# Which pairs take seven products, and where two on-chip columns are copied, in a two-layer encoder trunk

## The chip, the cores and the metric

One Trainium2 chip, one core. TensorE (PE) multiplies, PEld is its weight load, which runs beside it; VectorE (DVE), ScalarE (ACT) and GpSimd (POOL) prepare operands and combine results; SyncE (SP) issues loads. The metric is the device time of one execution, in microseconds, as a median of several runs.

## The reference

x is 256 tokens of 4096 float32 numbers, and there are two layers. A layer normalises x, multiplies it by w_in, runs attention and a retention on the parts, gates both, and multiplies by w_out; a last normalisation follows.

```python
for l in range(DEPTH):                       # DEPTH = 2
    h = rmsnorm(x, norm_w[l])                # (1, 256, 4096)
    proj = h @ w_in[l]                       # 4096 x 11264
    aq, ak, av, ag, rq, rk, rv, rg = jnp.split(proj, SPLIT_POINTS, axis=-1)
    ...                                      # rotary, softmax attention, both retentions, gates
    x = x + jnp.concatenate([a_out, r_out], axis=-1) @ w_out[l]   # 4096 x 4096
return rmsnorm(x, final_norm)
```

## The kernel before

The four large products are four stages: stage 0 is w_in of layer 0, stage 1 its w_out, stages 2 and 3 the same of layer 1. A w_in stage has 11 blocks of 1024 columns (two halves of 512), a w_out stage has four. Rows of a weight matrix come as 16 pairs of 128-row tiles. The work of one pair in one block is a 2 x 2 x 2 problem (two token halves, two k-tiles, two column halves), done in one of two ways:

- with eight products (an "eight"), from two weight pages, A and B;
- with seven (a "seven", from SEVEN_PRODUCTS at lines 160 to 170 of the kernel before), by a scheme like Strassen's, from four pages, A, T, B and U; T and U are sums of weights (`wsum`), which DVE forms in one addition of 128x1024 and two of 128x512.

Each product is one 128x128 by 128x512 product in float32 quality, made of three matmuls: high by high and low of the activations by high of the weights (line 1458), high of the activations by low of the weights (line 1468). So an eight is 24 matmuls and a seven 21. A page becomes a high part, `whi`, by a cast on ACT, and a low part, `wlo`, by a subtraction on DVE (`parts`, line 473). One page in some of the eights is "far": ACT makes `fhi` and its negative `flo`, and an accumulating DMA of POOL's queue adds the weights onto `flo`, so that DVE does nothing for it (`far_parts`). There are one buffer of `fhi` and `flo`, five of the other pages (RING), and five raw loads (RAWS) on SP's queue.

Products add up in seven banks, M1 to M7 (`M` in the rows). `combine` (line 1475) empties them at a block's end into `ca` and `cb`: one copy on ACT and seven additions on DVE. The last of them, ca with M4 or M2, frees the bank that the next block's products need early.

The program is written out by a planner in Python. It keeps clocks of its own (`ve`, `ac`, `now`; costs V_FIXED, S_FIXED, STEP_S, due times LANDING, STORE, FAR_LANDING, margins MARGIN, RUSH, EARLY, ADD_AHEAD, TIGHT_A, TIGHT_B) and between two products (`tick`, line 892) decides with `room` whether one more step of side work may be written at this place. So these constants only set the order of instructions on each engine, and the engines run it in that order.

Between layers, `out_task` (in lines 1518 to 1580) takes each column of 512 of layer 0's result: POOL adds the residual, ACT squares, DVE turns 32x32 blocks into `room`. Columns 0 to 5 go to DRAM and come back as operands. Columns 6 and 7 stay: `move` (line 939) copies `room` back on ACT in 16 copies of 32 partitions, into the tile of the result itself, which the store of x2 must have read by then.

In the profile a helper of line 247 records every instruction of DVE and ACT, so those are told apart by the names of tiles.

Of the kernel before, what the change touches and what calls it, by code (L numbers as in the profile page):

```python
# [12 lines left out]
F32R = mybir.dt.float32r  # L13
# [4 lines left out]
P = 128  # L18
D_MODEL = 4096
SEQ = 256  # L20
# [9 lines left out]
KG = 4  # L30
# [11 lines left out]
STEP_V = 1.6  # L42
STEP_S = 1.3

V_FIXED = 0.15
S_FIXED = 0.12
# [4 lines left out]
LANDING = 11.0  # L51
STORE = 8.0
FETCH = 13.0
FAR_LANDING = 11.0
MARGIN = 0.0

RUSH = 1.5

EARLY = 0.7

ADD_AHEAD = 2.5

# [3 lines left out]

TIGHT_A = 3
TIGHT_B = 5

# [21 lines left out]

FAR_PAIRS = (2, 5, 8, 11, 14)

# [77 lines left out]

SEVENS = (SEVEN, tuple(sorted(SEVEN + MORE)))
EIGHTS = [_p for _p in range(NP) if _p not in SEVENS[1]]

# [3 lines left out]
def pages_of(group, first=False):  # L178

    order, one = [], group[:1]  # L180
    rest = group[1:]
    if first:
        order += [(_p, _k) for _p in NATIVE if _p in group for _k in (PAGE_A, PAGE_B)]
        one = [_p for _p in one if _p not in NATIVE]
        rest = [_p for _p in rest if _p not in NATIVE]
    one = [(_p, _k) for _p in one for _k in (PAGE_A, PAGE_T, PAGE_B, PAGE_U)]
    rest = [(_p, _k) for _p in rest for _k in (PAGE_A, PAGE_B)]
    for _i, _v in enumerate(one):
        order += [_v] + rest[_i : _i + 1]
    return order + rest[len(one) :]  # L190


def is_far(group, p, k):

    return k == PAGE_B and p in FAR_PAIRS


def slots_of(group, second, first=False, plain=False):

    for _p, _k in pages_of(group, first):  # L200
        if _p in SEVENS[second] and not (first and _p in NATIVE):
            yield [(_b, _p, (ALL, _a), _k, _h) for _b, _a, _pg, _h in SEVEN_PRODUCTS if _pg == _k]
# [10 lines left out]
EASY = ("M7",)  # L213

TOGETHER = 4
BANKS = ("M1", "M2", "M3", "M4", "M5", "M6", "M7", "M8")

# [44 lines left out]
def hybrid_encoder(  # L262
# [136 lines left out]
    class Weights:  # L399


        def __init__(self):
            self.pages = []
            for l in range(DEPTH):
                for w, n in ((w_in, N_IN), (w_out, N_OUT2)):
                    for b in range(n):
                        second = w is w_out
                        for g in GROUPS[second]:
                            start = (l, b) == (0, 0) and w is w_in
                            for slot in slots_of(g, second, start):  # L410
# [3 lines left out]
                                one.seven = one.pair in SEVENS[second] and not one.whole  # L414
                                one.far = is_far(g, one.pair, one.kind) and not (
                                    start and (g in GROUPS[0][:2] or one.whole)
# [164 lines left out]
    def dead_room():  # L581

        if not rooms:
            e, o = len(EIGHTS), len(SEVENS[1])
            kinds = {
# [5 lines left out]
            }  # L591
            order = "x7h x7l x3 x3 x7h x7l x7h x7l x3 x8h x8l x7h x7l x3 x8h x8l x7h x7l x3 x7h" if MORE else "x3 x3 x8h x8l x3 x3 x8h x8l x7l x7h x3 x3 x8h x8l x3 x3 x8h x8l x7l x7h"
            rooms.extend(kinds[v] for v in order.split())
        tag, bufs, shape, flat = rooms.pop(0)
# [19 lines left out]
    def split_pair(p, v, whole, stage):  # L614
# [14 lines left out]
        x0, x1 = v[:, 0], v[:, 1]  # L629
        if p in SEVENS[stage % 2]:  # L630
            while sums_of or held[0] + pledged() >= PAGES:
# [3 lines left out]
            sums_of.append(p)  # L635
            hi = t(ap, [P, 7, P], "x7h", len(SEVENS[1]), F32R)
            lo = t(ap, [P, 7, P], "x7l", len(SEVENS[1]), F32R)
            f = page([P, 5, P], "xf")
# [15 lines left out]
        else:  # L654
# [5 lines left out]
            else:  # L660
                both = [t(ap, [P, 7, P], v, len(SEVENS[1]), F32R) for v in ("x7h", "x7l")]
                hi, lo = (v[:, 0:4, :].rearrange("p (i m) t -> p i (m t)", m=MT) for v in both)
# [24 lines left out]
        version[p] += 1  # L687
        operand[p] = (hi, lo) if p in SEVENS[stage % 2] else (hi, lo, g)
        operand_at[p] = max(ve.until, ac.until) + PASS
# [657 lines left out]
    def block(after_pair, phase, then, first_order=False, order=LAST_ORDER, last=None, plain=False, hurried=False):  # L1347
# [6 lines left out]
        flat = []  # L1354
        second = phase % 2 == 0
        rush[0] = RUSH if hurried else 0.0
        for g in GROUPS[second]:
            for slot in slots_of(g, second, first_order, plain):
                flat += slot
# [24 lines left out]
        def begin_product(n, name, p, index, k, h):  # L1384
# [18 lines left out]
            if first_order and p in NATIVE:  # L1403
                a = as_it_comes[p][0][:, index[0], index[1] * P : (index[1] + 1) * P]
            elif p in SEVENS[second]:
                a = at(operand[p], *index, ALL)
# [114 lines left out]
    def out_task(l, n, res):  # L1521
# [29 lines left out]
        else:  # L1551
            yield LANDING - 2.0
            to = res.rearrange("p m n -> p (m n)")
            yield from move(turn, to)
            drop()
            put(n, to, 2 * l + 2)

    def out_tasks(l, n, c):
        for i in range(2):
            nc.gpsimd.dma_start(c[i], residual(l, 2 * n + i), accum_op=ALU.add)  # L1560
        yield LANDING
        for i in range(2):
            yield from out_task(l, 2 * n + i, c[i])

# [242 lines left out]
```

## Time and profile before

| what | us |
|---|---|
| median of 3 runs | 2627.58 (2625.68 to 2627.82) |
| the profiled execution, its own time | 2625.96 |
| its span in the trace | 2623.8 |
| PE busy | 2601.0 (99%) |
| DVE busy | 2166.6 (83%) |
| ACT busy | 1804.2 (69%) |
| POOL busy | 372.9 (14%) |

The difference between the profiled execution's time and its span, 2.16 us, lies around the span. In the trace stage 0 ends near 985 us, stage 1 near 1317, stage 2 near 2280, and the last matmul of stage 3 starts at 2611.99. PE is nearly always busy, so its time is to be read by where its matmuls start later than one after another; the busy shares of the other engines tell how near they are to being late for it.

### The profile page before, as it was taken

How to read it: one execution, taken by the hardware profiler on the slowest of the kernel's cores; microseconds unless marked ns; L12 is line 12 of the kernel's file. 1: busy time of each engine (PE TensorE's matmuls, PEld its weight loads, DVE VectorE, ACT ScalarE, POOL GpSimd, SP SyncE). 2: the span in 40 equal slices, each digit the busy share in tenths (PEclk: the TensorE clock that was granted, in tenths of full speed). 3: DMA queues.
4: the chain of work that ended last, by engine and by line, in shares of the span. 5: the costliest groups of instructions: out<-in, count | busy, mean ns of one | idle time of the engine just before them, and what ended most of it. 6: DMA issues, size and time to landing. Idle time of an engine off the chain costs nothing.

```text
span 2623.8 us, 34532 instructions
## 1 busy us (share of the span) xinstructions
PE 2601.0 (99%) x11725; PEld 2154.2 (82%) x11725; DVE 2166.6 (83%) x2684; ACT 1804.2 (69%) x2576; POOL 372.9 (14%) x510
## 2 busy tenths in 40 slices
PE   9999999999999999999999999999999999999998
PEld 7788888888888888888878888888888888888886
DVE  7898887798778898877978878888887688987876
ACT  8676676667565788655877666776576557876655
POOL 0012211221111101111111111211210111010000
PEclk9999999999999999999999999999999999999999
DMA  9988888887778777889988888888877787788887
GB/s 305 285 262 285 272 271 284 270 269 243 235 238 249 239 249 237 274 262 281 311 246 259 271 274 283 266 273 288 280 231 217 245 258 239 221 259 264 254 249 228
DMA packets 201121, 683.94 MB, mean 261 GB/s; under 512 B 24176, under 2 KB 30832, under 8 KB 200944
## 3 DMA queue, kind: packets, MB, share of 16 engines
q1 hardware_dynamic: 147760, 521.27, 56.3%
q0 software_dynamic: 53184, 160.46, 26.5%
q8 instruction: 92, 1.51, 0.2%
q14 instruction: 85, 0.70, 0.1%
HBM read 637.60 MB, written 44.04 MB: 260 GB/s over the span
## 4 chain that ended last, share of the span: by engine, by line
PE 92%; issue 1%; DMA 1%; ACT 1%; DVE 1%; POOL 0%; POOLq 0%; DVEq 0%; ACTq 0%
PE M L1458 59%; PE M L1468 30%; PE ps L973 1%; PE ps L974 1%; PE ps L975 1%; DMA q<-q_dram 1%; PE ps L1458 0%; DMA wraw<-in_w_in 0%; DVE wlo L247 0%; ACT ca L247 0%; DVE ca L247 0%; PE ps L1468 0%; DVE cb L247 0%; ACT pr L247 0%; ACT whi L247 0%
## 5 line engine op out<-in xcount | busy, mean ns | idle before, releaser
L247 ACT CAST whi<-wraw 128x1024 fp32r<-128x1024 f32 (+1 forms) x808 | 768.7, 962 | 463.0 <-PE M L1458 310.3
L247 DVE TENSOR_TENSOR wlo<-wraw,whi 128x1024 fp32r<-128x1024 f32 (+1 forms) x808 | 886.9, 1110 | 236.6 <-ACT whi L247 230.9
L1458 PE MATMUL M<-whi,x8h 128*128 128x512 f32 x1340 | 521.9, 389 | 0.0
L1458 PE MATMUL M<-whi,x8l 128*128 128x512 f32 x1340 | 521.5, 389 | 0.0
L1458 PE MATMUL M<-whi,x7h 128*128 128x512 f32 x1265 | 493.9, 390 | 3.7 <-DVE ca L247 2.5
L1458 PE MATMUL M<-whi,x7l 128*128 128x512 f32 x1265 | 492.9, 390 | 0.0
L247 ACT CAST whi<-wsum 128x1024 fp32r<-128x1024 f32 x314 | 329.6, 1050 | 137.1 <-PE M L1458 93.8
L1468 PE MATMUL M<-wlo,x8h 128*128 128x512 f32 x1340 | 420.2, 389 | 0.0
L247 DVE TENSOR_TENSOR wlo<-wsum,whi 128x1024 fp32r<-128x1024 f32 x314 | 382.5, 1218 | 38.7 <-ACT whi L247 36.8
L1468 PE MATMUL M<-wlo,x7h 128*128 128x512 f32 x1265 | 407.8, 389 | 1.1 <-DVE wlo L247 1.1
L1458 PEld LDWEIGHTS M<-whi,x8h 128*128 128x128 f32 x1340 | 251.6, 188 | 51.7 <-issue 0.2
L1458 PEld LDWEIGHTS M<-whi,x8l 128*128 128x128 f32 x1340 | 251.6, 188 | 51.7 <-issue 0.2
L1468 PEld LDWEIGHTS M<-wlo,x8h 128*128 128x128 f32 x1340 | 251.2, 188 | 51.7
L1458 PEld LDWEIGHTS M<-whi,x7h 128*128 128x128 f32 x1265 | 237.8, 188 | 55.7 <-DVE ca L247 2.9
L1468 PEld LDWEIGHTS M<-wlo,x7h 128*128 128x128 f32 x1265 | 237.5, 188 | 50.5 <-DVE wlo L247 1.5
L1458 PEld LDWEIGHTS M<-whi,x7l 128*128 128x128 f32 x1265 | 238.0, 188 | 48.9
L1458 PE MATMUL M<-whi,x 128*128 128x512 f32 x840 | 258.9, 389 | 0.7 <-ACT whi L247 0.7
L505 POOL DMA_DIRECT2D flo<-in_w_in x108 | 97.3, 901 | 1044.4 <-ACT flo L247 1001.4
L247 ACT CAST fhi<-wraw 128x1024 fp32r<-128x1024 f32 (+1 forms) x148 | 154.7, 1045 | 99.8 <-PE M L1458 93.9
L247 DVE TENSOR_TENSOR wsum<-wraw 128x1024 f32<-128x1024 f32 x157 | 191.2, 1218 | 18.7 <-DMA wraw<-in_w_out 11.3
L1458 PEld LDWEIGHTS M<-whi,x 128*128 128x128 f32 x840 | 157.1, 188 | 32.9 <-ACT whi L247 1.1
L1458 PE MATMUL M<-fhi,x8h 128*128 128x512 f32 x440 | 171.3, 389 | 0.0
(301 smaller groups left out, 3282.9 us busy)
## 6 DMA issues: line engine op xcount, KB each, us to landing
wraw<-in_w_in SPq DMA_DIRECT2D x700, 512.0 KB, 5.0
wraw<-in_w_out SPq DMA_DIRECT2D x256, 512.0 KB, 5.2
flo<-in_w_in POOLq DMA_DIRECT2D x108, 512.0 KB, 7.9
flo<-in_w_out POOLq DMA_DIRECT2D x38, 512.0 KB, 8.8
full<-next_dram POOLq DMA_DIRECT2D x18, 512.0 KB, 7.7
p_dram<-room POOLq DMA_DIRECT2D x64, 128.0 KB, 4.6
pT<-p_dram POOLq DMA_DIRECT2D x16, 512.0 KB, 8.1
next_dram<-room POOLq DMA_DIRECT2D x40, 128.0 KB, 5.9
```

Of the source, the lines that this page charges most:

```text
L247: return call(out, *args, **kwargs)
L505: nc.gpsimd.dma_start(g.lo[h], g.src[0][:, h, :], accum_op=ALU.add)
L973: nc.tensor.matmul(out, a[0], b[0], start=start, stop=False)
L974: nc.tensor.matmul(out, a[0], b[1], start=False, stop=False)
L975: nc.tensor.matmul(out, a[1], b[0], start=False, stop=stop)
L1458: nc.tensor.matmul(acc[name], a[i], g.hi[h], start=m == first[name] and not i, stop=False)
L1468: nc.tensor.matmul(acc[name], a, g.lo[h], start=False, stop=m == final[name])
```

## The change

Before, the pairs 0, 3, 6, 9, 12 are sevens in the w_in stages, and 0, 1, 3, 6, 9, 12 in the w_out stages. After it each stage has a list of its own: 0, 3, 6, 9, 11 in stage 0, and 0, 3, 6, 9, 11, 13 in the others. The far pages are those of pairs 2, 5, 8, 12 and 14 in stage 0 and 2, 5, 8, 12 and 15 in the others (before: 2, 5, 8, 11, 14 in all). The on-chip columns 6 and 7 are copied from `room` to a page of their own, `to`, as soon as the turn is written, and column 7 is timed by its own residual. Constants of the planner change. The operands' tiles for retention rooms (`dead_room`) are listed pair by pair. The names TURNS, APART and ABREAST have values under which they change nothing.

```diff
-STEP_S = 1.3
-V_FIXED = 0.15
+STEP_S = 1.0
+V_FIXED = 0.08
...
-SEVEN = (0, 3, 6, 9, 12)
-MORE = (1,)
-DELAYED = tuple([_p for _p in range(NP) if _p not in SEVEN + MORE][-5:])
+SEVEN0 = (0, 3, 6, 9, 11)
+SEVEN1 = (0, 3, 6, 9, 11, 13)
+SEVEN2 = (0, 3, 6, 9, 11, 13)
+SEVEN3 = (0, 3, 6, 9, 11, 13)
+SEVENS = (SEVEN0, SEVEN1, SEVEN2, SEVEN3)
+MIXED = tuple(sorted(set(SEVEN0 + SEVEN1 + SEVEN2 + SEVEN3)))
+DELAYED = tuple([_p for _p in range(NP) if _p not in MIXED][-5:])
...
-FAR_PAIRS = (2, 5, 8, 11, 14)
+FAR0 = (2, 5, 8, 12, 14)
+FAR1 = (2, 5, 8, 12, 15)
...
+FARS = (FAR0, FAR1, FAR2, FAR3)
...
-def is_far(group, p, k):
-    return k == PAGE_B and p in FAR_PAIRS
+def is_far(stage, p, k):
+    return k == PAGE_B and p in FARS[stage] and p not in SEVENS[stage]
...
+OTHER = True
...
         else:
-            yield LANDING - 2.0
-            to = res.rearrange("p m n -> p (m n)")
-            yield from move(turn, to)
-            drop()
+            if OTHER:
+                yield 0.0
+                to = page([P, KG * SEQ], "to")
+                yield from move(turn, to)
+                drop(2)
+            else:
...
             put(n, to, 2 * l + 2)
 
     def out_tasks(l, n, c):
         for i in range(2):
             nc.gpsimd.dma_start(c[i], residual(l, 2 * n + i), accum_op=ALU.add)
-        yield LANDING
-        for i in range(2):
-            yield from out_task(l, 2 * n + i, c[i])
+            if i < 1:
+                yield APART
+        second = now.t + LANDING
+        yield max(0.0, LANDING - APART)
+        one = out_task(l, 2 * n, c[0])
+        if n < N_OUT2 - 1 or not ABREAST:
+            yield from one
+            yield max(0.0, second - now.t)
+            yield from out_task(l, 2 * n + 1, c[1])
+            return
```

How the order on the engines moves is shown at three places, each in the order of one engine's instructions. `x4` stands for four such instructions in a row.

First, ACT where stage 1 has passed into stage 2: `room` to `ca` are the copies of an on-chip column, `room,sums<-cb` the squares of the other column (cb is the second column of the last block). Before:

```order
L247 CAST whi<-wraw 128x1024 x2
L247 CAST whi<-wsum 128x1024
L247 COPY ca<-room 32x256 x8
L247 CAST whi<-wraw 128x1024
L247 COPY ca<-room 32x256 x4
L247 CAST whi<-wraw 128x512
L247 COPY ca<-room 32x256 x4
L247 CAST fhi<-wraw 128x1024
L247 ACTIVATE flo<-fhi 128x1024
L247 ACTIVATE room,sums<-cb 128x512 x2
L247 CAST whi<-wraw 128x1024
L247 CAST whi<-wsum 128x1024
```
After:

```order
L263 COPY to<-room 32x256 x4
L263 CAST whi<-wsum 128x1024
L263 COPY to<-room 32x256 x4
L263 CAST whi<-wraw 128x1024
L263 COPY to<-room 32x256 x4
L263 CAST whi<-wraw 128x1024
L263 CAST whi<-wsum 128x1024
L263 COPY to<-room 32x256 x4
L263 CAST whi<-wraw 128x1024
L263 CAST whi<-wraw 128x512
L263 ACTIVATE room,sums<-cb 128x512 x2
L263 ACTIVATE to<-to,nw 128x8x32 x4
```
Before, the 16 copies stand in runs of eight, four and four, and the squares of cb come behind them and behind a far page's `fhi` and `flo`. After, the copies (into `to`) stand in fours between casts, and the squares of cb come two casts behind the last of them, with no far page ahead.

Second, DVE at the end of the seventh block of stage 2 (columns of rg and rv; `D` and `wTl` belong to a retention, M_16482 is the bank that frees last). Before:

```order
L247 TENSOR_TENSOR cb<-ca,M_16566 128x512
L247 TENSOR_TENSOR ca<-cb,M_16450 128x512
L247 TENSOR_TENSOR wsum<-wraw,wsum 128x512
L247 TENSOR_TENSOR wsum<-wsum,wraw 128x512
L247 TENSOR_TENSOR wlo<-wsum,whi 128x1024
L247 TENSOR_TENSOR wTl<-D,wTh 128x1024
L247 TENSOR_TENSOR cb<-cb,M_16454 128x512
L247 TENSOR_TENSOR cb<-ca,M_16472 128x512
L247 TENSOR_TENSOR cb<-cb,M_16472 128x512
L247 TENSOR_TENSOR ca<-ca,M_16478 128x512
L247 TENSOR_TENSOR wlo<-wraw,whi 128x1024
L247 TENSOR_TENSOR ca<-ca,M_16482 128x512
```
After (that bank is M_16537 here):

```order
L263 TENSOR_TENSOR wlo<-wraw,whi 128x1024
L263 TENSOR_TENSOR wlo<-wsum,whi 128x1024
L263 TENSOR_TENSOR cb<-ca,M_16615 128x512
L263 TENSOR_TENSOR ca<-cb,M_16508 128x512
L263 TENSOR_TENSOR wlo<-wraw,whi 128x512
L263 TENSOR_TENSOR wTl<-D,wTh 128x1024
L263 TENSOR_TENSOR cb<-cb,M_16512 128x512
L263 TENSOR_TENSOR cb<-ca,M_16522 128x512
L263 TENSOR_TENSOR cb<-cb,M_16522 128x512
L263 TENSOR_TENSOR ca<-ca,M_16531 128x512
L263 TENSOR_TENSOR wlo<-wraw,whi 128x1024
L263 TENSOR_TENSOR ca<-ca,M_16537 128x512
```
The same combining additions stand there. After the change four `wlo` stand in the stretch where two stood, one of them the half page of a seven's page B, and the two `wsum` halves come before it.

Third, DVE at the end of the first block of stage 0. Before:

```order
L247 TENSOR_TENSOR wsum<-wraw 128x1024
L247 TENSOR_TENSOR wlo<-wraw,whi 128x1024
L247 TENSOR_TENSOR x_264<-x3f,x_264 128x256
L247 TENSOR_TENSOR wlo<-wraw,whi 128x1024
L247 TENSOR_TENSOR cb<-ca,M_457 128x512
L247 TENSOR_TENSOR ca<-cb,M_380 128x512
L247 TENSOR_TENSOR cb<-ca,M_372 128x512
L247 TENSOR_TENSOR cb<-cb,M_372 128x512
L247 TENSOR_TENSOR wsum<-wraw,wsum 128x512
L247 TENSOR_TENSOR wsum<-wsum,wraw 128x512
L247 TENSOR_TENSOR wlo<-wsum,whi 128x1024
L247 TENSOR_TENSOR x3f<-x8h 128x256
```
After:

```order
L263 TENSOR_TENSOR cb<-ca,M_454 128x512
L263 TENSOR_TENSOR ca<-cb,M_376 128x512
L263 TENSOR_TENSOR cb<-ca,M_368 128x512
L263 TENSOR_TENSOR cb<-cb,M_368 128x512
L263 TENSOR_TENSOR wsum<-wraw 128x1024
L263 TENSOR_TENSOR wlo<-wraw,whi 128x1024 x2
L263 TENSOR_TENSOR x3f<-x8h 128x256
L263 TENSOR_TENSOR x3f<-x8l 128x256
L263 TENSOR_TENSOR x3f<-x3f 128x256
L263 TENSOR_TENSOR wlo<-wraw,whi 128x1024
L263 TENSOR_TENSOR wsum<-wraw,wsum 128x512
L263 TENSOR_TENSOR wsum<-wsum,wraw 128x512
```
Before, the `wsum<-wraw` of the next block's first seven and the two `wlo` behind it stand ahead of the combining additions; after, the four additions of M6, M7 and M5 stand ahead of them. The last additions of M3 into cb come behind the rows shown in both, before with one x3f group between, after with two.

Counted over the program, 33 of the matmuls of 128x512 go (one product in each of 11 blocks). DVE gets 22 more `wlo<-wsum` of 128x1024, 11 more `wsum<-wraw` of 128x1024 and 22 more `wsum` of 128x512; ten `wlo` of 128x1024 become ten of 128x512. ACT gets 22 more `whi<-wsum` of 128x1024, and ten `whi` of 128x1024 become ten of 128x512. SP's loads stay as many, and POOL issues one more transfer.

## Rows read from the trace of the kernel before

**Rows 1.** Page, busy time and 40 slices of granted clock

```profile
PE 2601.0 (99%) x11725; PEld 2154.2 (82%) x11725; DVE 2166.6 (83%) x2684; ACT 1804.2 (69%) x2576; POOL 372.9 (14%) x510
...
PEclk9999999999999999999999999999999999999999
```
**Rows 2.** Chain that ended last: start us, us, what, xcount

```profile
188.41 1.81 PE M L1458 x8
```
**Rows 3.** Waits of PE: line, releaser: us in total, times, longest

```profile
PE M L1468 <- DVE wlo L247: 2.8, 2, 1.7
PE M L1458 <- DVE ca L247: 2.5, 3, 1.0
PE ps L973 <- ACT pr L247: 2.0, 2, 1.0
```
**Rows 4.** Timeline 84 to 103: start, duration, engine, operation, [wait, releaser]

```profile
88.39 1.05 ACT L247 CAST whi<-wraw 128x1024 fp32r<-128x1024 f32 x1 [4.52 <-DMA wraw<-in_w_in]
...
95.85 0.50 PE L1468 MATMUL M<-wlo,x7h 128*128 128x512 f32 x1 [1.06 <-DVE wlo L247]
...
97.58 0.50 PE L1458 MATMUL M<-whi,x7h 128*128 128x512 f32 x1 [1.23 <-DVE cb L247]
...
98.46 0.63 PE L1458 MATMUL M<-whi,x7h 128*128 128x512 f32 x1
...
101.45 0.52 PE L1458 MATMUL M<-whi,x7l 128*128 128x512 f32 x1
```
**Rows 5.** Timeline 1340 to 1362, ACT, DVE and PE

```profile
1343.20 3.32 ACT L247 COPY ca<-room 32x256 f32<-32x256 f32 x8
1353.66 0.61 ACT L247 ACTIVATE room<-cb 128x512 f32<-128x512 f32 x1
1355.01 0.17 DVE L247 TENSOR_REDUCE rstd<-sums 128x2 f32<-128x16 f32 x1 [4.37 <-ACT room L247]
1355.97 0.73 PE L1458 MATMUL M<-whi,x 128*128 128x512 f32 x2 [0.71 <-ACT whi L247]
1359.83 0.50 PE L1468 MATMUL M<-wlo,x 128*128 128x512 f32 x1 [1.75 <-DVE wlo L247]
```
**Rows 6.** Timeline 1314 to 1325, DVE: starts of instructions in a row

```profile
1315.18 0.68 DVE L247 TENSOR_TENSOR cb<-cb,M 128x512 f32<-128x512 f32 x1
1315.78 0.68 DVE L247 TENSOR_TENSOR ca<-ca,M 128x512 f32<-128x512 f32 x1
...
1322.79 1.22 DVE L247 TENSOR_TENSOR wsum<-wraw 128x1024 f32<-128x1024 f32 x1
1323.92 1.22 DVE L247 TENSOR_TENSOR wlo<-wraw,whi 128x1024 fp32r<-128x1024 f32 x1
```
**Rows 7.** Timeline 1927 to 1932: end of the seventh block of stage 2

```profile
1930.05 0.68 DVE L247 TENSOR_TENSOR ca<-ca,M 128x512 f32<-128x512 f32 x1
...
1931.92 0.39 PE L1458 MATMUL M<-whi,x7h 128*128 128x512 f32 x1
```
**Rows 8.** Windows: PE, PEld, DVE, ACT, POOL busy (x), clock, DMA share, GB/s

```profile
900.00:1000.00 100.00, 100.00 (x458) 83.24 (x457) 94.80 (x145) 83.20 (x137) 13.81 (x14) 1.00 0.72 227
...
2000.00:2100.00 100.00, 100.00 (x454) 83.27 (x453) 74.67 (x81) 60.05 (x69) 8.72 (x12) 1.00 0.74 230
```
**Rows 9.** Timeline 1329 to 1333: a far page is cast and sent, ACT and POOL

```profile
1329.91 1.05 ACT L247 CAST fhi<-wraw 128x1024 fp32r<-128x1024 f32 x1 [0.36 <-PE M L1458]
1331.00 1.06 ACT L247 ACTIVATE flo<-fhi 128x1024 fp32r<-128x1024 f32 x1
1332.35 0.86 POOL L505 DMA_DIRECT2D flo<-in_w_in  x1 [4.08 <-ACT flo L247]
```
**Rows 10.** Tile flo, 900 to 1000: its transfers

```profile
DMA to landing us min/median/max: 6.2/9.3/9.9
```
**Rows 11.** Tile flo, 2000 to 2100: its transfers

```profile
DMA to landing us min/median/max: 5.4/7.0/8.3
```
**Rows 12.** Timeline of PE at the end

```profile
2611.99 0.39 PE L1468 MATMUL M<-x7h,x8h 128*128 128x512 f32 x1
```

More of the change, by code (lines that the diff above doesn't have):

```diff
@@ L170 @@
 ]
-SEVENS = (SEVEN, tuple(sorted(SEVEN + MORE)))
-EIGHTS = [_p for _p in range(NP) if _p not in SEVENS[1]]
+EIGHTS = [_p for _p in range(NP) if _p not in MIXED]
 GROUPS = [[tuple(range(_a, _b)) for _a, _b in zip(_s, _s[1:] + (NP,))] for _s in SEVENS]
@@ L187, in pages_of, with slots_of @@
     rest = [(_p, _k) for _p in rest for _k in (PAGE_A, PAGE_B)]
+    turns = TURNS if group[-1] == NP - 1 else "0123"
     for _i, _v in enumerate(one):
-        order += [_v] + rest[_i : _i + 1]
-    return order + rest[len(one) :]
-def is_far(group, p, k):
-    return k == PAGE_B and p in FAR_PAIRS
-def slots_of(group, second, first=False, plain=False):
+        order += [_v] + [rest.pop(0) for _j in turns if _j == str(_i) and rest]
+    return order + rest
+def is_far(stage, p, k):
+    return k == PAGE_B and p in FARS[stage] and p not in SEVENS[stage]
+def slots_of(group, stage, first=False, plain=False):
     for _p, _k in pages_of(group, first):
-        if _p in SEVENS[second] and not (first and _p in NATIVE):
+        if _p in SEVENS[stage] and not (first and _p in NATIVE):
             yield [(_b, _p, (ALL, _a), _k, _h) for _b, _a, _pg, _h in SEVEN_PRODUCTS if _pg == _k]
@@ L213 @@
 EASY = ("M7",)
+APART = 0.0
 TOGETHER = 4
+OTHER = True
+TURNS = "0123"
+ABREAST = False
 BANKS = ("M1", "M2", "M3", "M4", "M5", "M6", "M7", "M8")
@@ L413, in __init__ @@
                                 one.whole = start and one.pair in NATIVE
-                                one.seven = one.pair in SEVENS[second] and not one.whole
-                                one.far = is_far(g, one.pair, one.kind) and not (
+                                one.seven = one.pair in SEVENS[stage] and not one.whole
+                                one.far = is_far(stage, one.pair, one.kind) and not (
                                     start and (g in GROUPS[0][:2] or one.whole)
@@ L591, in dead_room @@
             }
-            order = "x7h x7l x3 x3 x7h x7l x7h x7l x3 x8h x8l x7h x7l x3 x8h x8l x7h x7l x3 x7h" if MORE else "x3 x3 x8h x8l x3 x3 x8h x8l x7l x7h x3 x3 x8h x8l x3 x3 x8h x8l x7l x7h"
-            rooms.extend(kinds[v] for v in order.split())
+            for p in range(NP):
+                if p not in EIGHTS:
+                    rooms.extend(kinds[v] for v in ("x7h", "x7l"))
+                else:
+                    rooms.extend(kinds[v] for v in ("x3", "x8h", "x8l")[: 3 if p in EIGHTS[2:] and p not in DELAYED else 1])
         tag, bufs, shape, flat = rooms.pop(0)
@@ L1354, in block @@
         flat = []
-        second = phase % 2 == 0
+        stage = phase - 1
         rush[0] = RUSH if hurried else 0.0
-        for g in GROUPS[second]:
-            for slot in slots_of(g, second, first_order, plain):
+        for g in GROUPS[stage]:
+            for slot in slots_of(g, stage, first_order, plain):
                 flat += slot
@@ L1560, in out_tasks @@
             nc.gpsimd.dma_start(c[i], residual(l, 2 * n + i), accum_op=ALU.add)
-        yield LANDING
-        for i in range(2):
-            yield from out_task(l, 2 * n + i, c[i])
+            if i < 1:
[8 more added lines that the diff above has]
+            return
+        yield next(one)
+        yield max(0.0, second - now.t)
+        two = spawn(out_task(l, 2 * n + 1, c[1]))
+        yield from one
+        while not two.done:
+            yield 0.5
     def last_combine(res):
```

43 lines of the change are left out of this document (25 added, 18 removed).

## The prediction, made before the changed kernel ran

> **What bounds the kernel now.** I read the page first. PE is busy for 99% of the span and its clock stands at full in all 40 slices, while DVE has 83% and ACT 69% [rows 1]. The chain of waits agrees: its longest pieces are eight matmuls each, 1.81 us, so 0.226 us from one start to the next [rows 2]. A matmul that goes is therefore worth 0.226 us, as long as DVE and ACT still bring each page and free each bank in time. What PE loses now is in the waits of PE [rows 3] and, around them, in starts that lie further apart than 0.226 us. Start by start, less 0.226 us each, these places lose: about 4.7 us at the end of the first block, near 97; 1.0 at the end of the second, near 185; 4.6 in the attention of layer 0; 1.6 where stage 1 passes into stage 2, near 1317; 3.1 at 1356 to 1360; 1.1 where stage 2 passes into stage 3, near 2280; 1.4 at the start. That is 17.5 us of 2612, the whole that better order could give back. Then the timelines of the two largest places [rows 4, 5], DVE's spacing [rows 6], an end of a block in stage 2, where DVE gets the new work [rows 7], and the windows with the far pages' landings [rows 8, 10, 11].
>
> **What goes from PE.** 11 blocks of stage 2 lose one product of three matmuls: 33 x 0.226 = 7.5 us. All stand in PE's row of work, so they count in full where nothing else comes late. After the last matmul's start at 2611.99 [rows 12] 11.8 us of the span are left, and that end is written as before: 0.
>
> **What DVE and ACT get.** Starts in a row are 0.60 us apart for 128x512 and 1.13 for 128x1024 [rows 6]. DVE: 22 x 1.13 + 11 x 1.13 + 22 x 0.60, and 10 x (0.60 - 1.13), is 45.2 us, all in stage 2: 4.1 us for each of its blocks of some 87 us (stage 2 is 963 us). ACT gets 22 casts, at about 1.09 from one start to the next [rows 9] 24 us, less five for the halved ones: 1.7 us a block. DVE's share in stage 2 goes from about 83% to 88%. A stretch of 100 us near the start of stage 1 already has DVE at 94.8% with PE full throughout [rows 8], so as a share this fits. What hides it is DVE's idle time between pages; where that is gone is at the ends of blocks, below.
>
> **The copies of the on-chip columns.** Before, ACT runs eight copies from 1343.20 on, then four and four, then a far page, and starts the squares of cb only at 1353.66. DVE's first reduction behind them waits 4.37 us, to 1355.01, and the `wlo` in its queue behind that wait with it. PE then waits 0.71 us for a `whi` and 1.75 for a `wlo` [rows 5], and with the matmuls around them loses 3.1 us. After, no run of copies is longer than four, and the far page no longer stands ahead of the squares. DVE's wait goes, and of those behind it the `wlo` come in their turn. I take 3.1 off. Bounds: 0, if the squares are late by something else (column 7 now goes by its own residual), and 3.2, all that is lost there. The two orders differ at just the instructions that waited, so I take the end that these rows are near to.
>
> **The end of the first block.** A cast waits 4.52 us for a load at 88.39, DVE's subtraction waits for the cast, and all combining additions stand behind it; so PE waits 1.06 us for a `wlo` and 1.23 for a cb. From 98.46 to 101.45 its seven next starts are 0.43 apart, near the 0.427 of the clock's lower level, 1.2 GHz [rows 4]. After, four of the additions stand ahead of those weights. But the last two cb have one x3f group more between them. I expect about half, 2.5 us; bounds 0 and 4.8. The end of the second block follows with 0.5 of its 1.0 (0 to 1.0). Attention's waits (ACT `pr`, [rows 3], and others) are for its own chain, which is the same after: 0, bounds 2 more and 4.6 less, since side work around it is placed anew.
>
> **Ends of blocks in stage 2.** The bank freed last is needed by the next block's page B. In before, at the seventh block, ca with the last bank starts at 1930.05 and takes 0.68, and the product that needs it starts at 1931.92 [rows 7]: 1.2 us to spare. DVE's queue there, from the retention's last `D`, is 4 x 1.13 + 10 x 0.60 = 10.5 us, against 60 matmuls by 0.226 = 13.6 us on PE; after, 4 x 1.13 + 11 x 0.60 = 11.1 against 49 matmuls, 11.1: late by the time of handing over. Counted so, four further ends keep 1.1 us where they had 2.0 to 2.4, and six stay near 1.8 to 2.0. I add 1.5 us in stage 2: one end late by 0.5 to 1, and one or two of those with 1.1 late by a little. Bounds: 0, and the rival below. Where stage 1 passes into 2 and 2 into 3, the same count goes from 1.9 and 1.3 to 0.3; both places already wait on DVE's ca (2.5 us in three waits [rows 3]). I add 0.3 each, 0.6 together (0 to 3).
>
> **Far pages.** There is one buffer, so the next far page is cast only when PE has left the last. From there to its need stand mostly 65 matmuls, 14.7 us, before; after, 53 (12.0 us) in five blocks of stage 0, and 59 or 60 (13.5) in some sixteen others. The cast starts at 1329.91 and POOL issues at 1332.35 [rows 9]: 2.4 us. The median landing is 9.3 us with DVE at 94.8% [rows 8, 10] and 7.0 with DVE at 74.7% at nearly the same DMA share [rows 8, 11]. So 11.7 us against 12.0 at the median, and the longest, 9.9, is 0.3 late. I add 1.0: about three of the five late by 0.3. Bounds: 0, and 5 x 0.3 with 1.4 for the lower clock behind two of them, as in [rows 4], 4.3. By those rows 20 points of DVE's share go with 2.3 us of landing, so the 5 points in stage 2 give 0.6 us, which the 13.5 there hold.
>
> The Trainium skill, SBUF — State Buffer, section Who interferes with whom, says that the only contention is between VectorE and GpSimd over a shared port pair, and that DMA has ports apart from all engines. By that rule a busier DVE delays no landing, and the term for far pages in stage 2 is nothing; by the rows it is 0.6 us a page, inside the margin. The sum is the same by both, except in the slower rival, which it would make a little less likely. The trace agrees with neither firmly, since the two stretches also differ in what else they load.
>
> **Sum.** -7.5 - 3.1 - 2.5 - 0.5 + 1.5 + 0.6 + 1.0 = -10.5 us on the profiled execution's 2625.96: 2615.5. The median of the runs, 2627.58, lies 1.6 above that execution; on it, 2617.1. I say 2617.
>
> **Rivals.** A measurement of this kernel can tell 0.2%, 5.3 us: faster is under 2622.3, slower above 2632.8.
>
> *The saving is eaten by new waits.* All of the 7.5 us stands, the copies give their 3.1, but the first block gives nothing, and late banks and far pages cost 7 in all. For it: in stage 2 the end that I could follow has no spare time left, and five blocks of stage 0 have far pages within 0.3 us. Against it: the margins that the rows show were each above 1 us. Sum -7.5 - 3.1 + 7 = -3.6: 2624.
>
> *Nearly all waits go.* The planner's order holds everywhere: -7.5 - 3.1 - 4.8 - 1.0 and 1.3 to 2 of the other losses, with nothing added: -18, 2609.5. For it: block ends stay above 1 us at ten of eleven. Against it: three different places would have to come out at their best.
>
> *DVE becomes the bound at the ends of stage 2's blocks (slower).* The mechanism is the bank: DVE comes to ca with the last bank behind one `wlo` more, at each of the 11 ends. It decides as soon as DVE's queue at an end is longer by one 1.13 us subtraction than my count, for the 1.1 us that four ends have and the 1.2 that [rows 7] show are then gone. A wait like those of [rows 4], 1.2 us, and the matmuls at half clock behind it, 7 x 0.2 = 1.4, make 2.6 us an end; at the ends that have least (five) 13 us, at all eleven 29. With -7.5 - 3.1 that is 2630 to 2646; I say 2636. For it: the new work stands in DVE's queue just there, with DVE at 88%. Against it: [rows 8], 94.8% without a wait of PE, and the place near 1360, which lost only 0.6 us more than its two waits, so 2.6 is the dear end.
>
> The Trainium skill, TensorE: Matmul & The Clock Gate, Part 1, has the clock fall to half once PE has idled and come back when it is busy. The spacing of 0.43 at 98.46 agrees; near 1360 [rows 5] waits of 0.71 and 1.75 us cost little beside themselves, so a wait of that size need not bring it.
>
> That the change doesn't do what it says can be left out: the 33 matmuls are gone from the order of PE.
>
> **Chances.** My forecast 0.62, nearly all waits go 0.12, eaten 0.18, slower 0.08. Of my forecast's 0.62 some 0.04 reaches above 2622.3. The eaten case is within 0.2%, and a quarter of the slower case, whose cheap end is 2630, stays there too. So faster 0.62 - 0.04 + 0.12 = 0.70; same 0.04 + 0.18 + 0.02 = 0.24; slower 0.06. The range leaves out half of the best case and the dear half of the slower one: 2609 to 2630. My forecast's own range is 2611 to 2622.
>
> **What would show it.** PE's matmul count falls by 33, and stage 2 is about 6 us shorter. Near 1356 the waits for `whi` and `wlo` are gone, and DVE's reduction of rstd waits under 1 us. Near 97 one of the two waits is left, and the starts of 0.43 are fewer. In stage 2 the waits of PE show one to three on DVE's ca, under 1 us each, and in stage 0 perhaps three on flo. I am wrong if waits on ca or `wlo` come at most ends of stage 2, or if a new one of over 2 us shows in attention, or if the copies leave the squares as late as they were.

## The result, and the profile after

The changed kernel takes 2631.59 us (median of 14 runs, 2627.81 to 2635.59), the kernel before 2625.68 on the same chips (14 runs, 2621.0 to 2629.26): a ratio of 1.0024, 95% interval 1.0017 to 1.0031. The forecast was 2617, 0.4% faster. The profiled execution has a span of 2629.6 us against 2623.8.

The page and the chain of what ended last, by engine. PE is still busy for 99%, but DVE and DMA now hold 5% of the chain, where they held 2% before. The first two of these rows answer to [rows 1].

```profile
PE 2598.5 (99%) x11692; PEld 2149.6 (82%) x11692; DVE 2210.1 (84%) x2740; ACT 1829.4 (70%) x2599; POOL 367.1 (14%) x511
...
PEclk9999999999999999999999999999999999999999
...
PE 92%; DVE 3%; DMA 2%; ACT 1%; issue 1%; POOL 0%; DVEq 0%; SPq 0%; POOLq 0%; ACTq 0%
```
The waits of PE in the changed kernel: line, releaser: us in total, times, longest. They answer to [rows 3]. The waits on ACT's `pr` in attention are gone; waits on `flo`, on operands `x` and on DVE's ca are new or longer.

```profile
PE M L1477 <- DVE ca L263: 6.4, 5, 2.6
PE M L1487 <- DMA flo<-in_w_in: 4.2, 2, 3.3
PE M L1477 <- DVE x L263: 2.9, 2, 1.7
PE M L1487 <- DVE wlo L263: 1.8, 4, 0.9
PE M L1487 <- DMA flo<-in_w_out: 1.1, 1, 1.1
```
Worked out over all matmuls (start less the start before, less 0.2267 us, the usual distance of two starts), what PE loses at each place, in us:

| place (us in the span of before) | before | after | the forecast's term |
|---|---|---|---|
| end of the first block (60 to 115) | 4.5 | 1.2 | -2.5 |
| far page in the second block (115 to 150) | 0 | 5.2 | far pages +1.0 in all |
| end of the second block (150 to 320) | 1.3 | 0.1 | -0.5 |
| attention of layer 0 (320 to 560) | 4.9 | 0.6 | 0 |
| end of stage 0, blocks of stage 1 (960 to 1245) | 0.4 | 2.2 | none |
| last 70 us of stage 1 (1245 to 1316) | 0.1 | 5.0 | none |
| stage 1 into 2 (1316 to 1336) | 1.5 | 4.5 | +0.3 |
| on-chip columns (1336 to 1365) | 3.0 | 0 | -3.1 |
| operands x of stage 2 (1365 to 1420) | 0 | 1.9 | none |
| ends of blocks in stage 2 (1420 to 2240) | 0.7 | 1.9 | +1.5 |
| stage 2 into 3 (2240 to 2310) | 1.2 | 4.9 | +0.3 |
| operands x of stage 3 (2310 to 2390) | 0 | 2.3 | none |
| everywhere, the first 60 us too | 18.9 | 31.2 | |

So PE loses 12.3 us more, has 7.5 us of matmuls less, and the stretch behind its last matmul's start, 12.8 us, is 1.0 longer: +5.8, as the spans differ. The last matmul now starts at 2616.80, where [rows 12] had 2611.99.

A place in a single trace can differ from the next execution's by some 2.5 us. The trace of the kernel with one transfer moved (below), whose orders on PE, ACT, DVE and SP are the same as here, loses 2.7 us in attention where this one loses 0.6, and 2.5 in the last 70 us of stage 1 where this one loses 5.0. The passages between stages (4.8 and 4.8) and the operands x (2.3 and 2.0) agree in both.

**Where the on-chip columns are copied.** ACT and DVE: the last four copies, into `to`, come at 1348.78, the squares of cb at 1351.93, and DVE's reduction at 1353.29 shows no wait where [rows 5] had 4.37 us. PE waits for nothing between 1340 and 1362.

```profile
1348.78 1.65 ACT L263 COPY to<-room 32x256 f32<-32x256 f32 x4
...
1351.93 0.63 ACT L263 ACTIVATE room<-cb 128x512 f32<-128x512 f32 x1
...
1353.29 0.17 DVE L263 TENSOR_REDUCE rstd<-sums 128x2 f32<-128x16 f32 x1
```
**The far page in the second block.** POOL's queue, then PE: the transfer of `flo` is issued behind the four stores of vh and vl; PE waits 3.29 us for it, and behind it the starts from 129.51 to 132.92 lie 0.43 apart (3.41 us in eight steps); the granted clock there is 0.50, the lower of the two levels, as in [rows 4]. The row of the tile gives its landing, the longest of two, 12.1 us. The kernel before issues it ahead of the stores, which the first two rows show.

```profile
118.17 0.91 POOL L505 DMA_DIRECT2D flo<-in_w_in  x1 [3.70 <-ACT flo L247]
118.76 1.91 POOL L1281 DMA_DIRECT2D kv_dram<-vh  x2
```
The changed kernel:

```profile
113.27 1.59 POOL L1300 DMA_DIRECT2D kv_dram<-vh  x2 [1.06 <-ACT vh L263]
114.83 1.50 POOL L1300 DMA_DIRECT2D kv_dram<-vl  x2
116.30 0.97 POOL L521 DMA_DIRECT2D flo<-in_w_in  x1
...
128.48 0.50 PE L1487 MATMUL M<-flo,x8h 128*128 128x512 f32 x1 [3.29 <-DMA flo<-in_w_in]
...
129.51 0.62 PE L1477 MATMUL M<-whi,x7h 128*128 128x512 f32 x1
...
132.92 0.40 PE L1477 MATMUL ps<-whi,x8h 128*128 128x512 f32 x1
...
DMA to landing us min/median/max: 8.5/10.3/12.1
```
**The end of stage 2.** DVE, then PE. PE waits 2.57 us, for `ca<-cb,M`, which empties bank M7: the next block's second product is on M7. DVE runs from 2263.95 to 2284 without a gap, so that addition comes when its queue comes to it. Behind the wait the starts from 2279.99 to 2282.98 are 0.43 apart, at a granted clock of 0.50. In the kernel before M7 is emptied in time, and PE waits 0.86 us, for the last bank:

```profile
2274.50 0.69 DVE L247 TENSOR_TENSOR ca<-cb,M 128x512 f32<-128x512 f32 x1
...
2280.06 0.47 PE L1458 MATMUL M<-whi,x7h 128*128 128x512 f32 x1 [0.86 <-DVE ca L247]
```
The changed kernel:

```profile
2263.95 0.43 DVE L263 TENSOR_TENSOR full<-full 128x256 f32<-128x256 f32 x1
...
2276.97 0.68 DVE L263 TENSOR_TENSOR cb<-ca,M 128x512 f32<-128x512 f32 x1
2277.68 0.69 DVE L263 TENSOR_TENSOR ca<-cb,M 128x512 f32<-128x512 f32 x1
...
2278.51 0.47 PE L1477 MATMUL M<-whi,x7h 128*128 128x512 f32 x1 [2.57 <-DVE ca L263]
...
2279.99 0.63 PE L1477 MATMUL M<-whi,x7l 128*128 128x512 f32 x1
...
2282.98 0.55 PE L1477 MATMUL M<-whi,x8l 128*128 128x512 f32 x1
```
**Stage 1 into 2.** Here too PE waits for M7, 1.96 us. In the kernel before (first row) DVE empties it ahead of the sums of a seven's page U; in the changed kernel it does so behind them and their `wlo`.

```profile
1310.92 0.69 DVE L247 TENSOR_TENSOR ca<-cb,M 128x512 f32<-128x512 f32 x1
...
1318.60 0.69 DVE L263 TENSOR_TENSOR ca<-cb,M 128x512 f32<-128x512 f32 x1
...
1319.44 0.47 PE L1477 MATMUL M<-whi,x7h 128*128 128x512 f32 x1 [1.96 <-DVE ca L263]
```
**The seventh block of stage 2.** [rows 7] had 1.2 us to spare here. Now ca with the last bank is added at 1932.54, and PE waits 0.43 us for it: this term came as forecast.

```profile
1932.54 0.68 DVE L263 TENSOR_TENSOR ca<-ca,M 128x512 f32<-128x512 f32 x1
...
1933.28 0.50 PE L1477 MATMUL M<-whi,x8h 128*128 128x512 f32 x1 [0.43 <-DVE ca L263]
```
**The operands x.** DVE at the start of stage 3: the sums of a seven's page U (the second of the two is shown) and its `wlo` stand ahead of the split of the operand x that PE has been waiting for; the wait is 1.69 us.

```profile
2350.33 0.69 DVE L263 TENSOR_TENSOR wsum<-wsum,wraw 128x512 f32<-128x512 f32 x1
2350.93 1.22 DVE L263 TENSOR_TENSOR wlo<-wsum,whi 128x1024 fp32r<-128x1024 f32 x1
2352.07 0.75 DVE L263 TENSOR_TENSOR x8l<-ca,x8h 128x256 fp32r<-128x256 f32 x2
2352.86 0.42 DVE L263 TENSOR_TENSOR ca<-ca 128x256 f32<-128x256 f32 x1
2353.20 0.42 DVE L263 TENSOR_TENSOR x<-ca,x 128x256 fp32r<-128x256 f32 x1
...
2353.67 0.50 PE L1477 MATMUL M<-whi,x 128*128 128x512 f32 x1 [1.69 <-DVE x L263]
```

### The profile page after: what moved, and what is told of

Read it like the earlier page. It is cut to its first block, busy times and chain, and to the rows that moved or that the text cites. A ratio compares the mean times of both kernels' runs of the same rounds, so it can differ in the third digit from the quotient of the medians.

```text
span 2629.6 us, 34599 instructions
## 1 busy us (share of the span) xinstructions
PE 2598.5 (99%) x11692; PEld 2149.6 (82%) x11692; DVE 2210.1 (84%) x2740; ACT 1829.4 (70%) x2599; POOL 367.1 (14%) x511
## 4 chain that ended last, share of the span: by engine, by line
PE 92%; DVE 3%; DMA 2%; ACT 1%; issue 1%; POOL 0%; DVEq 0%; SPq 0%; POOLq 0%; ACTq 0%
PE M L1477 59%; PE M L1487 29%; DVE wlo L263 2%; PE ps L993 1%; PE ps L992 1%; PE ps L994 1%; DMA flo<-in_w_in 1%; DMA wraw<-in_w_in 1%; DVE wsum L263 1%; PE ps L1477 0%; PE M L1471 0%; DMA flo<-in_w_out 0%; ACT whi L263 0%; DVE cb L263 0%; PE ps L1487 0%
## 5 line engine op out<-in xcount | busy, mean ns | idle before, releaser
L263 DVE TENSOR_TENSOR wlo<-wsum,whi 128x1024 fp32r<-128x1024 f32 x336 | 409.5, 1219 | 119.3 <-ACT whi L263 118.7
L263 ACT CAST whi<-wsum 128x1024 fp32r<-128x1024 f32 x336 | 352.5, 1049 | 125.2 <-PE M L1477 93.5
L263 DVE TENSOR_TENSOR wsum<-wraw 128x1024 f32<-128x1024 f32 x168 | 204.5, 1217 | 15.3 <-DMA wraw<-in_w_out 10.8
L1477 PE MATMUL M<-fhi,x8l 128*128 128x512 f32 x438 | 170.5, 389 | 0.0
```

The lines of the kernel that those rows point to most:

```text
L263: return call(out, *args, **kwargs)
L1477: nc.tensor.matmul(acc[name], a[i], g.hi[h], start=m == first[name] and not i, stop=False)
```

## The experiments

All times stand beside runs of the kernel before on the same chip, the ratio with its interval. The changed kernel's is 1.0024. The kernel before took 2625.4 to 2626.8 us on the four chips used here. Two kernels' times on different chips are therefore uncertain by about 1 us, and with both intervals a difference of less than some 3 us is not clear of noise.

**Parts undone.** Four kernels. The first has the new lists and copies with the constants of before, the second the old lists with the new constants, the third only the copies, the fourth lacks the sixth seven of stage 2.

```diff
# e1_old_constants: the changed kernel with
-V_FIXED = 0.08      # and STEP_S, STORE, FAR_LANDING, MARGIN, RUSH, EARLY, ADD_AHEAD, TIGHT_A, TIGHT_B
+V_FIXED = 0.15      # all ten as before
# e2_old_lists
-SEVEN0 = (0, 3, 6, 9, 11)        # and SEVEN1 to 3, FAR0 to 3
+SEVEN0 = (0, 3, 6, 9, 12)        # all as before
# e3_copies_alone: both of these
# e4_stage2_five
-SEVEN2 = (0, 3, 6, 9, 11, 13)
-FAR2 = (2, 5, 8, 12, 15)
+SEVEN2 = (0, 3, 6, 9, 11)
+FAR2 = (2, 5, 8, 12, 14)
```

> The changed kernel with the ten planner constants of before (V_FIXED 0.15, STEP_S 1.3, STORE 8, FAR_LANDING 11, MARGIN 0, RUSH 1.5, EARLY 0.7, ADD_AHEAD 2.5, TIGHT 3 and 5); lists of sevens and copies are the new ones. Theory L (the new lists put sevens 11 and 13, and so DVE's work, near the ends of blocks, and DVE's queue is late at the ends of stages whatever the constants): the waits on DVE's ca near 1319 and 2278 and on wlo near 1290 stay, some 8 us more than before there, so 3 to 6 us slower than before. Theory C (the constants, V_FIXED above all, make the planner write more side work into the same time): those waits go, the copies and the 33 matmuls give their 7.5 + 3.1, so 8 to 11 us faster than before.

> The changed kernel with the lists of sevens and far pages of before; constants and copies are the new ones, and the 33 matmuls are back. Theory L: DVE's queue at the ends of stages 1 and 2 is as in the kernel before (waits of 1.0 each), the copies' 3.1 us and attention's 4.3 us are won, so 4 to 8 us faster than before although PE has all its matmuls. Theory C: the waits at the ends of stages and on far pages stay, with 7.5 us of matmuls back: 8 to 13 us slower than before.

Measured: 2658.26 us, 1.0124 (1.011 to 1.0138), and 2658.04 us, 1.0131 (1.0114 to 1.0149). Both theories were wrong in both: lists and constants each lose some 33 us without the other, and together 6. The waits of PE, of the first and of the second kernel, have a new largest row: an operand x that ACT casts too late, at the starts of stages 1 to 3. In both traces PE has to wait for the split of the last pairs, which stands behind other casts in ACT's queue.

```profile
PE M L1477 <- ACT x L263: 18.4, 4, 4.9
```
```profile
PE M L1477 <- ACT x L263: 12.3, 2, 6.4
```
The end of stage 2 loses 5.5 us with the new lists and old constants, and 4.9 with old lists and new constants; where both are old (third kernel) 1.1. So there either of them is enough, and the old lists have only five sevens in stage 2. Where stage 1 passes into 2 it is otherwise: new lists with old constants lose 3.8, old lists with new constants 0.2, where the kernel before loses 1.5. There it goes with the lists. The kernel before has six sevens in stage 1 as well, so it is not their number alone; the new list has sevens at pairs 11 and 13, close to the end of the block, where the old one has them at pairs 1 and 12.

> The changed kernel with lists and constants of before: only the copy of the on-chip columns to their own page is left of the change. Both theories: near 1356 the waits of PE (0.7 and 1.75 us) are gone, nothing else moves, 3 us faster than before. If the place is cured by the constants instead, it stays as it was: 0.

Measured: 2625.12 us, 1.0005 (0.9996 to 1.0013). In its trace PE waits for nothing near 1356, so the 3.0 us there are won by the copies alone. Over all places it loses 17.1 us instead of 18.9: the end of the second block and the last stage lose 2.5 more, attention 1.6 less. The interval goes from 1.0 us faster to 3.4 slower, so of the 3 us at this place nothing is seen in the time.

> The changed kernel with five sevens in stage 2 (0, 3, 6, 9, 11) as in stage 0: the 33 matmuls are back, and stage 2's DVE work is as before. If the sixth seven's DVE work is what makes DVE late at the end of stage 2, the 2.7 us wait near 2278 falls to about 1 and the time is 7.5 - 4.5 = 3 us above the changed kernel; if it is the lists' place or the constants, the wait stays and the time is 7.5 us above it.

Measured: 2632.76 us, 1.0028 (1.0018 to 1.0039). The 33 matmuls, 7.5 us, are back, and the time is only 1.2 us above the changed kernel's, clearly less than 7.5. The places tell why: stage 2 into 3 falls from 4.9 to 1.1, the operands x from 1.9 and 2.3 to 0 and 1.3, the ends of blocks from 1.9 to 0.8, 7.8 us in all. From 2262 to 2285 the only wait of PE left is this one:

```profile
PE M L1487 <- DMA flo<-in_w_in: 0.3, 1, 0.3
```
So most of what the sixth seven of stage 2 saves is given back at these places. The planner's whole order moves with it, and the far page of pair 15 becomes that of pair 14, so this run alone does not tell DVE's time from the order.

**One transfer moved.** In the second block the far page's `flo` goes ahead of the stores of vh and vl; the orders of PE, ACT, DVE and SP are the same to the row.

```diff
-            while self.adds and (now_all or self.adds[0][0] <= now.t + ADD_AHEAD):
+            while self.adds and (now_all or self.adds[0][0] <= now.t + (2.5 if now.t < 130.0 else ADD_AHEAD)):
```

> The changed kernel with one transfer moved: in the second block of stage 0 POOL sends the far page's flo before the four stores of vh and vl, as the kernel before does, instead of behind them. Nothing else of any engine's order changes. If the queue is why this flo lands 12.1 us after its issue and PE waits 3.3 us for it at 128, the wait falls below 1 and the clock stays up behind it: 4 to 5 us faster than the changed kernel, 2626 to 2628. If the window of 53 matmuls is too short for any landing there, the wait stays above 2 and the time falls by less than 1.5.

Measured: 2627.22 us, 1.0002 (0.9993 to 1.0011), so 4.4 us less than the changed kernel (5.5, each set less its own runs of before). POOL's queue and the landing in this kernel:

```profile
116.17 0.91 POOL L521 DMA_DIRECT2D flo<-in_w_in  x1 [3.71 <-ACT flo L263]
116.76 1.91 POOL L1300 DMA_DIRECT2D kv_dram<-vh  x2
118.30 1.84 POOL L1300 DMA_DIRECT2D kv_dram<-vl  x2
...
DMA to landing us min/median/max: 7.9/8.0/8.0
```
The transfer is issued at 116.17, 0.13 us earlier than in the changed kernel, and lands 8.0 us later instead of 12.1; the wait of 3.29 us is gone and so are the slow starts behind it (115 to 150 loses 0.6). It is the place in the queue, not the short window. The Trainium skill, DMA: Bandwidth & Descriptors, section Queues, rings and completion order, says in its paragraph on the queues of SyncE and ScalarE that on each DMA engine descriptors are consumed in ring order. It says so of those two queues; this pair of runs shows a transfer held up by those ahead of it on POOL's.

**One seven less in stage 1.**

```diff
-SEVEN1 = (0, 3, 6, 9, 11, 13)
-FAR1 = (2, 5, 8, 12, 15)
+SEVEN1 = (0, 3, 6, 9, 11)
+FAR1 = (2, 5, 8, 12, 14)
```

> The changed kernel with five sevens in stage 1 (0, 3, 6, 9, 11; far pages 2, 5, 8, 12, 14): 12 matmuls, 2.7 us, come back, and DVE loses 4 times 4.1 us of work at the ends of stage 1's blocks. If the seven of pair 13 is what makes DVE late before the end of stage 1, the waits on wlo from 1287 to 1311 and on ca and cb near 1320 go (some 8 us with the clock) and the time falls by 4 to 6 us, to about 2626. If the split of the next stage's operands alone fills DVE there, most of the waits stay and the time rises by 1 to 3 us.

Measured: 2630.66 us, 1.0015 (1.0007 to 1.0024), 0.9 less than the changed kernel with 2.7 us more of matmuls. Stage 1 into 2 falls from 4.5 to 0.2 and the blocks of stage 1 from 1.4 to 0; but the 70 us ahead of that only from 5.0 to 3.4, and the operands x of stage 2 rise from 1.9 to 4.5. The passage from stage 1 to 2 is cured, here and in all later kernels with five sevens in stage 1. For the other two places one trace is not enough: the first kernel under "Cures put together", with the same orders on PE, ACT, DVE and SP, loses 4.9 and 1.9 there. In this kernel DVE empties M7 at 1307.46, where the changed kernel does at 1318.60, so less work and an earlier place in the queue go together here.

**DVE's time for the `wlo` of sums halved, its order kept.** This kernel leaves out the low part of the pages T and U.

```diff
-                    ve.tensor_sub(g.lo[h], src[:, h, :], f32(g.hi[h]))
+                    if g.cheap:        # pages T and U of stages 1 to 3
+                        ve.until = max(ve.until, now.t) + vector_cost("tensor_sub", 2 * NB, {})
+                        nc.vector.tensor_copy(g.lo[h], f32(g.hi[h]))
+                    else:
+                        ve.tensor_sub(g.lo[h], src[:, h, :], f32(g.hi[h]))
```

> The changed kernel, every engine's order unchanged, with DVE's wlo of pages T and U in stages 1 to 3 written by a copy of whi in place of the subtraction (this leaves out the low part of these weights): each takes about 0.6 us in place of 1.13. If DVE's time is what sets the waits at the ends of stages 1 and 2 and on the operands x, those on DVE (11 us by the waits, some 18 with the clock behind them) nearly all go, and the time falls by 10 to 16 us, to 2616 to 2621; stage 0 keeps its 5 us at 128. If they are set by transfers or by ACT, they stay and the time falls by less than 3 us.

Measured: 2621.8 us, 0.998 (0.9968 to 0.9991) of the kernel before, 9.8 us below the changed kernel. These `wlo` on DVE from 1300 us on (228 in all), and the waits of PE:

```profile
L504 DVE CAST wlo<-whi x182: 648/687/768, 1300.6 to 2593.0; 128x1024 fp32r<-128x1024 f32 x182
...
PE M L1482 <- DVE ca L263: 2.8, 3, 1.6
...
PE M L1482 <- DVE x L263: 1.2, 1, 1.2
```
Waits on DVE's ca fall from 6.4 to 2.8 us and on x from 2.9 to 1.2; stage 2 into 3 loses 2.2 instead of 4.9, stage 2's starts and ends 1.7 instead of 3.8. So DVE's time decides in stage 2. Stage 1 into 2 keeps 4.2 of its 4.5, so the time of these `wlo` is not the answer there. In the changed kernel ACT waits 2.20 us there for a load of stage 2's first pages, and DVE's next `wlo` and the additions stand behind that cast. But DVE is idle for only 0.24 us before that `wlo` (0.69 here), so the load is not shown to be the answer either. Whether the same work with M7 emptied earlier in DVE's order would cure it was not run. The row is ACT's, in the changed kernel.

```profile
1312.87 1.05 ACT L263 CAST whi<-wraw 128x1024 fp32r<-128x1024 f32 x1 [2.20 <-DMA wraw<-in_w_in]
```
**Cures put together.** The first has the moved transfer and five sevens in stage 1. The second has four far pages in stage 0. The third asks besides for more room before side work, the fourth is the third with five sevens in stage 1, the fifth the first with five sevens in stage 2 as well.

```diff
# e9_four_far_pages; e10 and e11 have these too
-FAR0 = (2, 5, 8, 12, 14)
-ADD_AHEAD = 0.5
+FAR0 = (2, 5, 8, 14)
+ADD_AHEAD = 2.5
# e10_more_margin, e11_more_margin_five
-STEP_V = 1.6
-STEP_S = 1.0
-MARGIN = 0.2
-TIGHT_A = 4
+STEP_V = 1.75
+STEP_S = 0.8
+MARGIN = 0.4
+TIGHT_A = 5
```

> The changed kernel with the far page of the second block sent first and five sevens in stage 1, the two cures so far (4.4 and 0.9 us) in one kernel. If their places are independent, the time is 2631.6 - 5.3 = 2626, level with the kernel before. If a cure at one place only shifts the loss to the next (the operands x near 1390 took 4.3 us in the kernel with five sevens), it is above 2628.

Measured: 2626.26 us, 0.9996 (0.9987 to 1.0005): as the two cures add up.

> The changed kernel with four far pages in stage 0 (2, 5, 8, 14) and ADD_AHEAD 2.5 throughout, so that flo goes ahead of stores everywhere. If stage 0's far pages come late because of the queue and the short window, 4 to 6 us faster than the changed kernel, 2626 to 2628, and no wait on flo over 1 us. If DVE in stage 0 is as short of time as in stage 2, the 11 more wlo it gets (12 us) show as waits on ca at the ends of blocks, and the time is not below 2629.

Measured: 2626.76 us, 1.0001 (0.9992 to 1.0009), 4.8 less than the changed kernel. From 60 to 960 no wait on flo is left, and of the ends of blocks there none waits on ca for the `wlo` that DVE got; stage 0 into 1 and attention each lose 1.3 us more than in the changed kernel. This trace is of an execution of 2631.0 us, one of the two longest, which loses 2.2 us more in its first 60 us, so its places do not add up to the gain of the median.

> As the kernel with four far pages, and with more room asked for before side work is written (MARGIN 0.4, STEP_V 1.75, TIGHT_A 5; STEP_S 0.8): all lists of sevens stay. If the losses at the ends of stages come from side work written too close to them, the waits on DVE's ca near 1320 and 2278 fall and the time is 2618 to 2624, below the kernel before. If DVE has no time left there at all, they stay and the time is as with four far pages.

> As the one with more margin, with five sevens in stage 1: 2.7 us of matmuls come back. If the end of stage 1 still loses 6 us there, it goes and the time falls by 2 to 4 us against the one with more margin; if that had cured it, the time rises by 1 to 3 us.

Measured: 2632.0 us, 1.002 (1.0011 to 1.0029), and 2628.99 us, 1.0005 (0.9996 to 1.0014). More margin cures neither passage: from 2275 to 2300 PE still loses 4.8 us, from 1300 to 1325 5.7. With five sevens in stage 1 the latter falls to 1.1, and the time by 3.0. The kernel with more margin is 5.2 us slower than the one with four far pages on the same chip; their traces, of executions of 2630.1 and 2631.0 us, do not show where.

> The changed kernel with the far page of the second block first and five sevens in stages 0, 1 and 2: 45 matmuls, 10.2 us, more than the changed kernel, 12 more than the kernel before. If the sixth seven's DVE work is what PE waits for at the ends of stages 1 and 2 and on the operands x behind them, those waits (some 5 us near 1300, 5 near 2275, 4 near 1390 and 2350 with the kernels that have six) are gone and the time is 2624 to 2627, level with the kernel before with more matmuls. If they belong to the planner's constants, they stay and the time is 2634 or more.

Measured: 2626.39 us, 0.9998 (0.9989 to 1.0007), with 45 matmuls, 10.2 us, more than the changed kernel, and level with the kernel with the moved transfer alone (0.8 less, not clear of noise). In this kernel's waits of PE no row on an operand x is left, and those on ca are four short ones:

```profile
PE M L1487 <- DVE wlo L263: 3.1, 5, 0.9
PE M L1487 <- DMA flo<-in_w_out: 2.7, 1, 2.7
PE M L1477 <- DVE ca L263: 2.5, 4, 0.9
```
Stage 1 into 2 loses 0 and stage 2 into 3 loses 0.7. What stays are the last 70 us of stage 1, 7.8 us, on `wlo` and on a far page. No kernel here was faster than the kernel before, apart from the one that leaves work out.

## Why the prediction was wrong, step by step

**What came as forecast.** The 33 matmuls went (7.5 us). The copies gave 3.0 at their place for the 3.1 forecast. The end of the first block gave 3.3 for 2.5, that of the second 1.2 for 0.5. In the first block the size is right by luck: I expected one of the two waits to stay, but both are gone (4.5), and a new one of 0.92 us, for a far page at 88.17, takes 1.1 back. Ends of blocks inside stage 2 cost 1.2 for 1.5, 0.7 of it at the end named. Attention gave 4.3 where I had put 0 with that bound. The kernel with the copies alone still loses 3.3 there, the first two under "Parts undone" 0.2 each, but the one with a moved transfer 2.7; what of the 4.3 is the change and what is this execution stays open.

**The step that failed** is the one on where stage 1 passes into 2 and 2 into 3: "I add 0.3 each, 0.6 together (0 to 3)". They cost 3.0 and 3.7 more, with the lower clock behind them, and the operands x behind each passage 1.9 and 2.3, which had no term at all: 10.9 in place of 0.6 (11.3 in the trace of the kernel with the moved transfer). I had counted DVE's queue from an instruction that PE releases to the addition of the last bank. Two things were wrong with that. The wait came for the bank of M7, the second one in DVE's order of additions, since the next block's second product is on M7; and DVE did not stand idle when the count began: at the end of stage 2 it had been busy without a gap for 14 us and more, with the sums, the `wlo` and the split of the next stage's operands. Inside stage 2 the count came out right; DVE is busy for 77.7% there between 2000 and 2100, so it has time to catch up between ends.

The runs show that at the end of stage 2 DVE's time decides: halve the time of the sums' `wlo` without moving an instruction, and more than half of the loss goes (4.9 to 2.2); take the sixth seven away, and nearly all the excess goes (4.9 to 1.1). So most of the 7.5 us of the sixth seven is paid back in DVE's time. It is not the only way to be late there, since the old lists under the new constants lose 4.9 at that place with five sevens. Where stage 1 passes into 2, halving left 4.2 of 4.5 and five sevens left 0.2 or less; the loss goes with the list of sevens there, and whether by DVE's work or by the place of M7's addition in its order stays open. In the forecast this was the rival in which "DVE becomes the bound", at 0.08; it named the 11 ends of stage 2's blocks, with 2.6 us each. It came true at the last of them, where DVE also splits the next stage's operands, and hardly at the others (0.7 at the seventh).

**The term that was mis-sized** is far pages: +1.0 (0 to 4.3), measured 5.2 at one page (the 1.1 of the first block is counted above). I had looked at windows and landings, and not at POOL's own queue, where this page is now issued behind four stores; moved ahead of them it lands 8.0 us after its issue in place of 12.1, the place loses 4.6 us less, and 4.4 us of time come back. The weighing of DVE's load against landings was beside the point: DVE is busier in both windows of [rows 8], 95.9 and 77.7%, and the median landings, of six transfers each, fall from 9.3 and 7.0 us [rows 10, 11] to 8.6 and 6.5. So the 0.6 us that I took from two windows does not show. The Trainium skill, SBUF — State Buffer, section Who interferes with whom, says that DMA never contends with a compute engine; for transfers that GpSimd issues, as these are, it names an exception, that GpSimd can be starved while it writes their descriptors, which the prediction left out. No sign of that exception shows in these medians. The rows of the changed kernel, windows first, then the landings in the same two:

```profile
900.00:1000.00 100.00, 99.60 (x462) 83.00 (x461) 95.89 (x154) 86.65 (x149) 13.08 (x16) 1.00 0.83 250
...
2000.00:2100.00 100.00, 100.00 (x454) 83.27 (x453) 77.74 (x86) 63.07 (x75) 8.93 (x12) 1.00 0.78 239
```
```profile
DMA to landing us min/median/max: 8.1/8.6/10.4
...
DMA to landing us min/median/max: 5.5/6.5/9.6
```
The share of DMA is 0.83 and 0.78 there, so the two kernels do not differ in DVE alone.

**What stays open.** What holds M7's addition back where stage 1 passes into 2 is open, as said above. The last 70 us of stage 1 lose 5.0 us, on `wlo` and on far pages. The kernels with five sevens in stage 1 lose from 3.2 to 7.8 there and the one with halved `wlo` of sums 2.5, but so does the one that moved nothing but a transfer of stage 0; only with old lists and old constants together (third kernel) is it gone. The 1.0 us behind the last matmul has no explanation here. And the constants: with the lists of before they cost 33 us, and the old ones cost as much with the new lists; no run tells which of the ten does it.

By the sum: the forecast's -10.5 had to be corrected by +10.3 for the passages and operands, +4.2 for the far page, +4.9 for the end of stage 1, +1.8 for the end of stage 0 and the blocks of stage 1, +1.0 at the end, and by -4.3 for attention and -1.5 for the first two blocks, which makes +5.9; the spans differ by 5.8.

## What to carry to other kernels

A matmul taken off a PE that is busy 99% of the time is worth its time only where the engine that pays for it has time left. In this case that is read from the stretch with the most side work (the passage from stage 2 to 3), not from the share over a stage. When following an end of a block, begin where the engine was last idle, and look for the first bank that is needed, not only for the last that is freed. When a planner's numbers change, read every queue's order, POOL's too: one transfer behind four stores cost as much as 19 matmuls.

## What the runs showed of the hardware that was not expected

A transfer of 512 KB issued on POOL's queue right behind four stores landed 12.1 us after its issue, and 8.0 when issued ahead of them. Behind waits of PE of 3.29 and 2.57 us the granted clock was 0.50 and the starts of matmuls were 0.43 apart for 3.4 and 3.0 us, so that these places cost 5.2 and 4.9 us in all.
